# A hybrid decoder trunk on one core: other delays for the key and value compression, another share of filler products per head, and half of the small evictions on ScalarE

## The chip, the cores and the metric

The kernel runs on one core of one Trainium2 chip. The metric is the device time of one execution in microseconds (us). The kernel before takes 641.56 us, the median of three runs (640.89 to 641.58).

## The reference

Two layers over 256 tokens of width 1024, in float32. Layer 0 mixes a short convolution with latent attention, layer 1 is sparse attention with 16 heads in 4 groups; a squared-ReLU MLP follows each. The change touches the attention of layer 1, cut here to what matters:

```python
proj = xn @ w_in                       # q, and k/v of three branches, and gates
def compress(z, pe, w1, w2):           # blocks of 32 tokens, every 16
    blk = z[:, idx] + pe[:, None, :]
    hdn = jax.nn.gelu(jnp.einsum('bnlgd,lde->bnge', blk, w1))
    return hdn @ w2
kc, vc = compress(k_c, pe_k, w1_k, w2_k), compress(v_c, pe_v, w1_v, w2_v)
# each head: softmax over the 15 compressed blocks, over the selected blocks, over the window
out = g0 * softmax(q.kc - alibi) @ vc + g1 * softmax(q.ks - alibi) @ vs + g2 * softmax(q.kw - alibi) @ vw
return out @ w_out
```

With 256 tokens the 16 selected blocks are all four blocks there are, and the window covers everything, so those two branches are dense causal softmaxes.

## The kernel before

A dense product is three TensorE products: each operand is split into a high part (fp32r) and a low part, and high by high, high by low and low by high are summed in PSUM. A weight chunk (512 KB) is loaded by SP's queue into one of 4 `raw` buffers, its high part is copied by ScalarE (L170) and its low part subtracted by VectorE (L171), both into one of 5 `w` buffers.

TensorE's instructions run in the order in which the program issues them. That order is planned by hand with a clock (`tick`, L62): each product adds its planned duration (L91), 256 columns 109 ns. `defer(ns, fn)` (L75) puts a group of instructions off until the clock has moved on by that much; `need` (L83) forces what is still deferred when it is needed. The order on the other engines is chosen by the framework's scheduler; what stands in a `high_priority` block is preferred.

`mixer_c` (L671) is layer 1's attention. Four projections have their output turned (`turned_steps`, L349: a step is six products of 256 columns, 16 steps a projection, one epilogue two steps before the end, for the first half of the outputs, and one at the end): the keys (L821), the first query pair (L827), and then, as filler between the heads, "c" (the inputs of both compressions, L859) and "q" (the second query pair, groups 2 and 3, L860). After these the list of fillers holds the products of the output projection (`out_steps`), which wait for attention results.

- `epi_c(i)` (L774) scales the projection into `z[i]` (VectorE, L778), copies the lower half of the partitions to the upper half, one token on, by a DMA (L779), and defers `fold(i)`.
- `fold(i)` (L784) issues the compression's eight products (`compress`, L649, planned at 143 ns each), whose short chain on VectorE and ScalarE makes gelu's result (hk or hv), and defers `last_k` or `last_v`, the second product.
- `epi_q(1)` (L758) scales by VectorE (sp, L744) and writes the high and low parts of the queries qT (ScalarE L768, VectorE L769).

The head loop (L981) has 32 heads in slots 0 to 31, in units (gp, t) of eight heads: t is the half of the queries, t = 0 sees 128 keys, t = 1 sees 256. In a slot:

- `head_qk` (L895) makes the scores of both branches in one of two `sc` PSUM buffers; two fused passes on VectorE add the bias and take the maximum (L911), ScalarE exponentiates (L913), VectorE inverts the sum (L915), GpSimd scales (L918);
- what the table `at` holds for this slot: `scores_c` (L966, products with the compressed keys, then a chain of VectorE and ScalarE operations to the tile cpc, L1010 to L1027, and 6000 ns later by the clock the four transposes of cpc and ptc), `unit_pv` (L939, probabilities by values) and `unit_end` (L954, which forces the transposes of cpc of its unit and adds the compressed branch);
- `fill(FILL[i])` (L877): filler steps as long as the credit is positive; a debt is carried to the next slot, and credit that finds no filler ready is lost;
- `head_t` (L926): the transposes of the head four slots back, 2 blocks for t = 0 and 4 for t = 1, whose result is evicted from PSUM by VectorE for t = 0 (L935) and by ScalarE for t = 1 (L937).

The score chain of the first unit:

```python
s3 = ...                      # VectorE: reduce, add the bias, maximum, subtract
nc.scalar.activation(s3, s3, AF.Exp)
...                           # VectorE: sum, reciprocal, gate, scale
nc.scalar.activation(pc[:, :, 0:4:2, :], wide, AF.Copy)
nc.vector.tensor_tensor(pc[:, :, 1:4:2, :], wide, pc[:, :, 0:4:2, :].bitcast(F32), op=OP.subtract)
```

Of the kernel before, what the change touches and what calls it, by code (L numbers as in the profile page):

```python
# [39 lines left out]

LAG = 4
C_TILES = 2 * C_HEADS
FILL = (1900.0,) * 6 + (1200.0,) * 10 + (300.0,) * 5 + (700.0,) * 11 + (1200.0,) * 8


class Trunk:
# [624 lines left out]
    def mixer_c(self, x, rx, both, fin):  # L671
        nc, A = self.nc, self.A
        with ExitStack() as st:
# [16 lines left out]
            def wide(i):  # L690

                return rows[i].rearrange("p t n -> p (t n)")[:, None, :].to_broadcast([P, 2, 256])
# [81 lines left out]
            def epi_c(i, ps):  # L774
                with self.tc.high_priority():
                    for par in range(2):
                        rows_ = slice(64 * par, 64 * par + 64)
                        nc.vector.tensor_tensor(z[i][0:64, par:4:2, :], ps[rows_], wide(0)[rows_], op=OP.mult)  # L778
                    nc.sync.dma_start(z[i][64:128, 0:4, 0:S - 1], z[i][0:64, 0:4, 1:S])  # L779
                self.defer(5500.0 + 2500.0 * i, lambda: fold(i))  # L780

            cps = []

            def fold(i):  # L784
                if i == 0:
                    cps.append(self.acc(0))
                    self.compress(qp, cps[0][:, 0:80], z[0], w1[0], "ck", out_k)
                    self.defer(4500.0, last_k)
                else:
                    self.compress(qp, cps[0][:, 80:160], z[1], w1[1], "cv", out_v)  # L790
                    self.defer(4500.0, last_v)

            def out_k(xx, y):
                nc.vector.tensor_tensor(hk, xx, y, op=OP.mult)
# [62 lines left out]
            def always():  # L857
                return True
            fills = [("c", always, self.turned_steps(both, "c_in", 0, epi_c)),  # L859
                     ("q", always, self.turned_steps(both, "c_in", 3, epi_q(1))),  # L860
                     ("o", mixed(0, 0), out_steps(0, 0, (0, 1))),
# [15 lines left out]
            def fill(ns):  # L877
                credit[0] += ns
                while credit[0] > 0:
                    if not fills or not fills[0][1]():  # L880
                        credit[0] = 0.0
                        return
                    was = self.clk
                    step()
                    credit[0] -= self.clk - was
# [36 lines left out]
            def head_t(*a):  # L922
                with self.tc.high_priority():
                    head_t_(*a)

            def head_t_(gp, g, t, r, pb):  # L926
                n = 2 * (t + 1)
                if r == 0:
                    pts[g, t] = qp.tile([P, 4, 4, P], F32, name="pt", tag="pt", bufs=3)[:, 0:n]
                ph = pts[g, t]  # L930
                pt = self.trp()
                for b in range(n):
                    self.tr(pt[:, b, :], pb[:, b * P:(b + 1) * P])
                if t == 0:
                    nc.vector.tensor_copy(ph[:, :, r, :], pt[:, 0:n, :])  # L935
                else:
                    nc.scalar.activation(ph[:, :, r, :], pt[:, 0:n, :], AF.Copy)  # L937

            def unit_pv(gp, t):  # L939


                nb = t + 1
                y = yps[gp, t] = (self.acc(1) if (gp, t) != (1, 1) else
                                  pp.tile([P, 512], F32, name="sc", tag="sc", bufs=2))
                with self.tc.high_priority():
                    for b in range(2 * nb):
                        br, kb = b // nb, b % nb
                        for par in range(2):
                            self.mm(y[64 * par:64 * par + 64, :],
                                    vv[kb][:, br * 2 + gp, 64 * par:64 * par + 64],  # L950
                                    pts[2 * gp + par, t][:, b].rearrange("p a b -> p (a b)"), b == 0, False, 2,
                                    part=True)

            def unit_end(gp, t):  # L954

                with self.tc.high_priority():
                    self.need(lambda: (gp, t) in ptc)
                    self.mm(yps[gp, t], vcs[:, gp, :], ptc[gp, t], False, True, part=True)
                    mh, ml = self.xt_both(mixed_, gp, t)
                    y = yps[gp, t].rearrange("p (a b) -> p a b", a=4)  # L960
                    nc.scalar.activation(mh, y, AF.Copy)
                    nc.vector.tensor_tensor(ml, y, mh.bitcast(F32), op=OP.subtract)
                    mixT[t][gp] = (mh, ml)
                    ready[t, gp] = self.clk + 1500.0

            def scores_c(gp, t):  # L966
                self.need(lambda: left[0] == 2)
                fns = self.cmp_scores(qp, pp, [q and q[:, :, t] for q in qT], kc, cbias[:, t], gates[t], gp, t, ptc)
                self.defer(6000.0, fns[0])

            units = [(0, 0), (0, 1), (1, 0), (1, 1)]
            at = {}
            for u, i in enumerate((13, 16, 23, 29)):
                at.setdefault(i, []).append(lambda u=u: scores_c(*units[u]))
            for u in range(4):
                at.setdefault(8 * u + 8 + LAG, []).append(lambda u=u: unit_pv(*units[u]))
                at.setdefault(max(8 * u + 8 + LAG, 17), []).append(lambda u=u: unit_end(*units[u]))

            fill(2200.0)
            prob = {}  # L980
            for i in range(C_TILES + LAG + 4):  # L981
                now[0] = i
                if i < C_TILES:
                    gp, g, t, r = heads[i]
# [3 lines left out]
                for fn in at.get(i, []):  # L988
                    fn()
                fill(FILL[i])  # L990
                j = i - LAG
# [217 lines left out]
```

## Time and profile before

| | |
|---|---|
| median of three runs | 641.56 us |
| the profiled execution | 639.43 us, its span 637.6 us |
| TensorE busy | 617.9 us, 97% of the span |
| VectorE busy | 423.2 us, 66% |
| ScalarE busy | 375.0 us, 59% |
| GpSimd busy | 78.6 us, 12% |
| mean granted TensorE clock | 0.991 of full |

The profile names an engine (PE is TensorE, DVE VectorE, ACT ScalarE, POOL GpSimd, SPq SyncE's queue of DMA issues), the line of the kernel and the tiles that an instruction writes and reads (out<-in). Products that are issued by a helper all have its line (L92, L99, L104), so they are told apart by their tiles: acc<-z_k is the K compression, acc<-xth a filler product, sc<-qT a head's scores, sc<-kc the compressed scores, acc<-pt,vv the product of probabilities and values, tr<-cpc the transposes of the compressed probabilities. An instruction's duration on TensorE overlaps the next one's; the distance of two starts is what it costs. The attention of layer 1 begins near 320 us; its head loop runs from about 352 to 440.

### The profile page before, as it was taken

To read this page: it belongs to the slowest core of one execution; us is meant where nothing else is said; L and a number is where in the kernel's file an instruction comes from. 1 tells how busy PE (TensorE), PEld (TensorE's weight loads), DVE (VectorE), ACT (ScalarE), POOL (GpSimd) and SP (SyncE) were. 2 spreads that over 40 slices of the span, in tenths; PEclk is the share of its full clock that TensorE was granted. 3 is DMA by queue.
4 is the path that set the end of the run, shared out by engine and by line. 5 is a ranking of instruction groups with operands and counts; after the bars stand their busy time and mean duration, and the time that the engine had idled before them with its cause. 6 is when DMAs were issued, how large, how long until landed. Compare 5 with 4: busy or idle time off the path is not lost.

```text
span 637.6 us, 10525 instructions
## 1 busy us (share of the span) xinstructions
PE 617.9 (97%) x3712; PEld 536.6 (84%) x3712; DVE 423.2 (66%) x975; ACT 375.0 (59%) x860; POOL 78.6 (12%) x135
## 2 busy tenths in 40 slices
PE   7999999999999999999899897999999999999995
PEld 4889877889999988888899886776789999888884
DVE  6758797776676744445968789584966675644443
ACT  5786556756665644445857568596756565544431
POOL 1212330020000000000200535360300000000000
PEclk9999999999999999999999998999999999999998
DMA  8856336646556566566688814023636656556521
GB/s 279 292 180 218 129 101 197 219 146 199 185 178 197 168 208 192 194 198 211 198 271 262 219 47 133 1 68 106 222 105 206 190 174 203 188 193 198 197 69 66
DMA packets 33796, 111.67 MB, mean 175 GB/s; under 512 B 4240, under 2 KB 5328, under 8 KB 33744
## 3 DMA queue, kind: packets, MB, share of 16 engines
q1 hardware_dynamic: 33744, 111.01, 53.5%
q8 instruction: 29, 0.48, 0.3%
q14 instruction: 23, 0.19, 0.1%
HBM read 108.38 MB, written 1.05 MB: 172 GB/s over the span
## 4 chain that ended last, share of the span: by engine, by line
PE 60%; issue 28%; DVE 6%; ACT 2%; DMA 2%; POOL 1%; SPq 0%; DVEq 0%; POOLq 0%; ACTq 0%
PE acc L92 52%; PE sc L92 4%; PE tr L99 4%; DVE wlo L171 2%; ACT pbn L913 1%; DMA raw<-in_a_in 1%; DMA z_k<-z_k 1%; DVE xtl L254 1%; PE yp L92 1%; DVE X L292 1%; POOL rp L139 0%; DVE xlo L171 0%; DVE pst L282 0%; DVE pbn L911 0%; POOL rx L139 0%
## 5 line engine op out<-in xcount | busy, mean ns | idle before, releaser
L171 DVE TENSOR_TENSOR wlo<-raw,whi 128x512 fp32r<-128x512 f32 (+3 forms) x368 | 237.5, 683 | 127.1 <-ACT whi L170 125.0
L170 ACT ACTIVATE whi<-raw 128x512 fp32r<-128x512 f32 (+3 forms) x362 | 207.1, 617 | 139.8 <-PE acc L92 87.8
L92 PE MATMUL acc<-xtl,whi 128*128 128x256 f32 x512 | 143.8, 281 | 0.0
L92 PE MATMUL acc<-xth,whi 128*128 128x256 f32 x512 | 143.5, 280 | 0.0
L92 PE MATMUL acc<-xth,wlo 128*128 128x256 f32 x512 | 143.5, 280 | 0.0
L92 PE MATMUL acc<-whi,hl 128*128 128x512 f32 x256 | 99.8, 390 | 0.0
L92 PE MATMUL acc<-whi,hh 128*128 128x512 f32 x256 | 99.6, 389 | 0.0
L92 PE MATMUL acc<-wlo,hh 128*128 128x512 f32 x256 | 99.6, 389 | 0.0
L92 PEld LDWEIGHTS acc<-xth,whi 128*128 128x128 f32 x512 | 96.3, 188 | 1.0 <-issue 0.8
L92 PEld LDWEIGHTS acc<-xth,wlo 128*128 128x128 f32 x512 | 96.7, 189 | 0.1
L92 PEld LDWEIGHTS acc<-xtl,whi 128*128 128x128 f32 x512 | 96.2, 188 | 0.2
L92 PE MATMUL acc<-wlo,xth 128*128 128x512 f32 (+3 forms) x160 | 60.3, 379 | 1.3 <-DVE wlo L171 1.1
L92 PE MATMUL acc<-whi,xth 128*128 128x512 f32 (+3 forms) x160 | 60.3, 377 | 0.7 <-DVE whi L166 0.7
L92 PE MATMUL acc<-whi,xtl 128*128 128x512 f32 (+3 forms) x160 | 60.5, 378 | 0.0
L92 PEld LDWEIGHTS acc<-wlo,hh 128*128 128x128 f32 x256 | 48.1, 188 | 10.0
L92 PEld LDWEIGHTS acc<-whi,hl 128*128 128x128 f32 x256 | 48.1, 188 | 9.9
L92 PEld LDWEIGHTS acc<-whi,hh 128*128 128x128 f32 x256 | 48.1, 188 | 9.8
L139 POOL TENSOR_TENSOR rp<-mse,mhalf 128x1 f32<-128x1 f32 x8 | 5.1, 643 | 387.5 <-DVE mse L136 387.5
L918 POOL TENSOR_SCALAR pbn<-pbn,sm,gates 128x128 f32<-128x128 f32 (+1 forms) x64 | 39.6, 630 | 72.9 <-PE acc L92 39.8
L92 PEld LDWEIGHTS acc<-wlo,xth 128*128 128x128 f32 x160 | 30.0, 188 | 7.2 <-DVE wlo L171 2.7
L92 PEld LDWEIGHTS acc<-whi,xth 128*128 128x128 f32 x160 | 30.2, 189 | 5.6 <-ACT xth L252 1.1
L92 PEld LDWEIGHTS acc<-whi,xtl 128*128 128x128 f32 x160 | 30.1, 188 | 4.4
(237 smaller groups left out, 854.8 us busy)
## 6 DMA issues: line engine op xcount, KB each, us to landing
raw<-in_w SPq DMA_DIRECT2D x128, 512.0 KB, 4.3
raw<-in_c_in SPq DMA_DIRECT2D x16, 512.0 KB, 4.6
raw<-in_a_in SPq DMA_DIRECT2D x15, 512.0 KB, 4.5
raw<-in_a_out SPq DMA_DIRECT2D x8, 512.0 KB, 3.6
raw<-in_c_out SPq DMA_DIRECT2D x8, 512.0 KB, 3.9
raw<-in_a_qup SPq DMA_DIRECT2D x6, 384.0 KB, 3.5
gpost<-in_gpost SPq DMA_DIRECT2D x4, 512.0 KB, 3.8
bias<-in_bias SPq DMA_DIRECT2D x4, 512.0 KB, 4.1
```

Source lines behind the costliest of these rows:

```text
L92: self.nc.tensor.matmul(ps, a, b, start=start, stop=stop, **({"skip_group_check": True} if part else {}))
L99: self.nc.tensor.transpose(dst, src, self.ident)
L139: nc.gpsimd.tensor_tensor(r, e, self.mhalf, op=OP.pow)
L170: nc.scalar.activation(hi[:, sl], raw[:, sl], AF.Copy)
L171: nc.vector.tensor_tensor(lo[:, sl], raw[:, sl], hi[:, sl].bitcast(F32), op=OP.subtract)
L254: nc.vector.scalar_tensor_tensor(lo, src, gcol, hi.bitcast(F32), OP.mult, OP.subtract)
L292: nc.vector.scalar_tensor_tensor(self.X[t][:, sl], self.tmp.pop(0), r, self.X[t][:, sl], OP.mult, OP.add)
L913: nc.scalar.activation(pb[:, sl], pb[:, sl], AF.Exp, bias=nm[:, br:br + 1], scale=-1.0, accum_out=sm[:, br:br + 1])
L918: nc.gpsimd.tensor_scalar(pb[:, sl], pb[:, sl], sm[:, br:br + 1], gates[t][:, 1 + br, h:h + 1], OP.mult, OP.mult)
```

## The change

The planned delays from `epi_c` to the compressions grow from 5500 and 8000 ns to 8000 and 10300; those from a compression to its second product from 4500 to 5800 (K) and 5500 (V). The list of filler credits is 1500 for eight slots, 1250 for nine, 500 for four, and then as before, in place of 1900 for six, 1200 for ten and 300 for five. The first `scores_c` stands in slot 14 instead of 13, the first `unit_end` in slot 18 instead of 17. The evictions of t = 0 stay on VectorE for odd r and go to ScalarE for even r.

```diff
@@ -40,7 +40,7 @@
 
 LAG = 4
 C_TILES = 2 * C_HEADS
-FILL = (1900.0,) * 6 + (1200.0,) * 10 + (300.0,) * 5 + (700.0,) * 11 + (1200.0,) * 8
+FILL = (1500.0,) * 8 + (1250.0,) * 9 + (500.0,) * 4 + (700.0,) * 11 + (1200.0,) * 8
 
 
 class Trunk:
@@ -777,7 +777,7 @@
                         rows_ = slice(64 * par, 64 * par + 64)
                         nc.vector.tensor_tensor(z[i][0:64, par:4:2, :], ps[rows_], wide(0)[rows_], op=OP.mult)
                     nc.sync.dma_start(z[i][64:128, 0:4, 0:S - 1], z[i][0:64, 0:4, 1:S])
-                self.defer(5500.0 + 2500.0 * i, lambda: fold(i))
+                self.defer(8000.0 + 2300.0 * i, lambda: fold(i))
 
             cps = []
 
@@ -785,10 +785,10 @@
                 if i == 0:
                     cps.append(self.acc(0))
                     self.compress(qp, cps[0][:, 0:80], z[0], w1[0], "ck", out_k)
-                    self.defer(4500.0, last_k)
+                    self.defer(5800.0, last_k)
                 else:
                     self.compress(qp, cps[0][:, 80:160], z[1], w1[1], "cv", out_v)
-                    self.defer(4500.0, last_v)
+                    self.defer(5500.0, last_v)
 
             def out_k(xx, y):
                 nc.vector.tensor_tensor(hk, xx, y, op=OP.mult)
@@ -931,7 +931,7 @@
                 pt = self.trp()
                 for b in range(n):
                     self.tr(pt[:, b, :], pb[:, b * P:(b + 1) * P])
-                if t == 0:
+                if t == 0 and r % 2:
                     nc.vector.tensor_copy(ph[:, :, r, :], pt[:, 0:n, :])
                 else:
                     nc.scalar.activation(ph[:, :, r, :], pt[:, 0:n, :], AF.Copy)
@@ -970,11 +970,11 @@
 
             units = [(0, 0), (0, 1), (1, 0), (1, 1)]
             at = {}
-            for u, i in enumerate((13, 16, 23, 29)):
+            for u, i in enumerate((14, 16, 23, 29)):
                 at.setdefault(i, []).append(lambda u=u: scores_c(*units[u]))
             for u in range(4):
                 at.setdefault(8 * u + 8 + LAG, []).append(lambda u=u: unit_pv(*units[u]))
-                at.setdefault(max(8 * u + 8 + LAG, 17), []).append(lambda u=u: unit_end(*units[u]))
+                at.setdefault(max(8 * u + 8 + LAG, 18), []).append(lambda u=u: unit_end(*units[u]))
 
             fill(2200.0)
             prob = {}
```

## Rows read from the trace of the kernel before

**Rows 1.** waits of TensorE over the whole run: us in total, times, longest

```profile
PE tr L104 <- DVE cpc L1027: 2.4, 1, 2.4
PE acc L92 <- DMA z_k<-z_k: 2.0, 1, 2.0
...
PE sc L92 <- DVE nm L911: 0.9, 2, 0.6
PE acc L92 <- ACT ptc L1035: 0.7, 1, 0.7
...
PE acc L92 <- DVE cct L659: 0.7, 1, 0.7
```

**Rows 2.** busy us (x instructions) of each engine in five stretches, then PEclk, DMA share, GB/s

```profile
356.10:380.60 24.50, 21.79 (x167) 20.63 (x165) 19.48 (x80) 13.47 (x47) 9.11 (x15) 1.00 0.46 126
380.60:394.70 14.10, 10.73 (x71) 8.07 (x69) 13.53 (x51) 12.83 (x39) 7.48 (x11) 0.99 0.44 136
394.00:396.00 2.00, 0.75 (x4) 0.56 (x4) 1.77 (x10) 2.00 (x10) 1.71 (x3) 0.58 0.47 182
396.20:400.70 4.50, 4.50 (x20) 4.09 (x20) 2.77 (x15) 2.73 (x7) 1.19 (x3) 0.50 0.02 5
401.00:440.00 39.00, 39.00 (x200) 26.49 (x198) 24.65 (x100) 26.01 (x82) 16.02 (x28) 1.00 0.16 52
```

**Rows 3.** timeline of TensorE, 363 to 399 us: start us, us, instruction, [idle before it and its releaser]

```profile
363.99 2.46 PE L92 MATMUL acc<-z_k,cw 128*128 128x80 f32 x16 [1.99 <-DMA z_k<-z_k]
...
380.27 0.28 PE L92 MATMUL acc<-xth,wlo 128*128 128x256 f32 x1
...
381.17 2.05 PE L92 MATMUL acc<-pt,vv 128*64 128x512 f32 x8
...
384.67 0.60 PE L99 MATMUL tr<-ident,pbn 128*128 128x128 f32 x4
385.02 0.48 PE L92 MATMUL sc<-kTh,qT 128*128 128x512 f32 x1
...
385.57 0.96 PE L92 MATMUL sc<-kc,qT 128*128 128x32 f32 x8
386.38 0.66 PE L99 MATMUL tr<-ident,pbn 128*128 128x128 f32 x4
...
394.68 0.75 PE L104 MATMUL tr<-ident_r,cpc 128*128 128x128 f32 x4 [2.37 <-DVE cpc L1027]
...
396.71 1.05 PE L99 MATMUL tr<-ident,pbn 128*128 128x128 f32 x4
...
397.99 1.05 PE L99 MATMUL tr<-ident,pbn 128*128 128x128 f32 x4
```

**Rows 4.** timeline of VectorE, the query epilogue and the end of the score chain

```profile
382.04 0.69 DVE L744 TENSOR_TENSOR sp<-acc,row 128x512 f32<-128x512 f32 x1
...
383.50 1.60 DVE L769 TENSOR_TENSOR qT<-sp,qT 64x512 fp32r<-64x512 f32 x2
...
392.32 1.59 DVE L769 TENSOR_TENSOR qT<-sp,qT 64x512 fp32r<-64x512 f32 x2 [0.24 <-ACT qT L768]
...
394.21 0.42 DVE L1027 TENSOR_TENSOR cpc<-cs,cpc 128x256 fp32r<-128x256 f32 x1
```

**Rows 5.** timeline of the DMA queue (SyncE), the issue of the first z copy

```profile
358.11 0.65 SPq L779 DMA_DIRECT2D z_k<-z_k  x1
```

**Rows 6.** DMA issues by line, 320 to 420 us: times, KB each, median us to landing

```profile
z_k<-z_k SPq DMA_DIRECT2D x1, 255.0 KB, 5.8
```

**Rows 7.** groups of instructions by form, 356 to 396 us: busy us, mean ns | idle before

```profile
L913 ACT ACTIVATE pbn<-pbn,nm 128x256 f32<-128x256 f32 x16 | 8.0, 504 | 2.3 <-DVE nm L911 1.4 <-DVE sm L915 0.7
L171 DVE TENSOR_TENSOR wlo<-raw,whi 128x512 fp32r<-128x512 f32 x11 | 7.5, 690 | 0.3 <-ACT whi L170 0.3
...
L911 DVE CUSTOM_DVE_ANT_0 pbn<-sc,bias 128x256 f32<-128x256 f32 x16 | 6.3, 412 | 0.1
...
L935 DVE COPY pt<-tr 128x256 f32<-128x256 f32 x8 | 3.4, 419 | 1.1 <-PE tr L99 0.9
```

## The prediction

> **What bounds the kernel now.** I read the waits of TensorE first, since its order is written out by hand and it is the engine that is nearly always busy. Five of its waits lie close together, between 356 and 397 us, in the first half of layer 1's heads: 2.4 us for the last operation of the compressed-score chain (cpc), 2.0 for the copied z_k, 0.9 for a score buffer that VectorE still reads (twice), 0.7 for ptc, 0.7 for hk [rows 1]. The sum is 6.7 us. The windows then say which engine is short there [rows 2]: from 356.1 to 380.6 VectorE works 19.48 of 24.50 us, so it has 5.0 to spare; from 380.6 to 394.7 it works 13.53 of 14.10, ScalarE 12.83, and TensorE 10.73. The first waits are thus TensorE arriving too early with VectorE idle beside it; the last and longest is VectorE being late. There is a second cost: after the cpc wait the granted clock is 0.58 of full between 394 and 396 and 0.50 (1.2 GHz) until 400.7. From 401 to 440 TensorE is busy all 39.00 us [rows 2], so whatever is won before 401 is carried to the end.
>
> The timelines give the instants. The first z_k product waits 1.99 us until 363.99; the first half of the second query pair's products ends at 380.39; scores_c(0,0) runs from 385.57 to 386.38; the transposes of cpc begin at 394.68 after their 2.37 us of idleness [rows 3]. On VectorE the first query epilogue runs from 382.04 to 385.10, the second's last operation ends at 393.91, cpc at 394.63 [rows 4].
>
> **The order that the change makes.** A fill step is six 256-column products, planned at 109 ns each (256/2.4 + 2.5), 655 ns in all; a slot takes steps as long as its credit is positive and carries the debt on. After four steps ahead of the loop, slots 0 to 12 took 3,3,3,2,3,3,2,2,0,2,2,1,2 and slots 13 on nothing (28 steps; deferred groups charge their own time to the credit). With the new list slots 0 to 14 take 2,2,3,2,2,3,2,2,2,0,2,0,2,2,2. So head 4 is issued before the first compression epilogue instead of after, and heads 12 and 13, the first product of unit (0,0) and its four-transpose slot come before the first half of the second query pair ends. scores_c(0,0) goes from slot 13 to 14, the forced transposes of cpc from slot 17 to 18. By slot 15 the planned totals are equal again.
>
> **Cost, step by step**, against the profiled execution (639.43 us, span 637.6).
>
> *z_k.* TensorE stood before the compression at 362.0 (363.99 less 1.99 [rows 3]), which the plan puts 5.6 us after the epilogue's last product, so that product ended near 356.4; the copy was issued at 358.11 [rows 5] and took 5.8 us [rows 6], to 7.6 us after the product. Now 56 fill products, four heads and four pairs of transposes lie between, planned 8.1 us. The wait goes, with half a microsecond to spare: -2.0 there. Bounds: 0 (the copy is held on SP's in-order queue behind a c_out load that waits for a raw buffer) and -2.0; I take -2.0, since at 358.11 nothing held it.
>
> *hk.* Between the K compression and last_k the plan had 4.5 us and now has 5.9, against a wait of 0.7. It goes too: -0.7.
>
> *What these two are worth.* They are won at a place where VectorE is idle, and what ends last is VectorE at cpc. TensorE reached the end of the first query half at 380.4. It now has in front of that point the pv products of unit (0,0) (381.17 to 383.15, 2.0), two more four-block heads (385.02 to 385.57, 0.55 each) and one more slot of four transposes (384.67 to 385.02, 0.35) [rows 3], 3.45 us; head 4 falls out for a pair of transposes, 0.2 each way; the epilogue comes 0.2 later. 380.4 + 3.45 + 0.2 - 2.7 gives 381.4, hardly later than before. But more of VectorE's work is then behind it. Before, 13.5 us of work lay between there and cpc [rows 2]. Of that the second half of head 11's softmax, heads 12 and 13 (two passes of 0.41 each [rows 7], with a reciprocal some 0.9 a head) and one eviction of 0.42 are done by then: 2.3 us, using the 5.0 that were idle. 381.4 + 13.5 - 2.3 = 392.6 for cpc, against 394.63. A second way: the chain took from 386.38 to 394.63, 8.2 us, on a full VectorE; scores_c(0,0) now ends at 381.4 plus the rest of slot 13 and the head of 14 (eleven products 1.2, transposes 0.35, head 0.55, scores 0.81 [rows 3]), 384.3, and 384.3 + 8.2 = 392.5. Both say -2.1. TensorE without any wait would be there at about 389.1, so some 3.4 us of waiting stay.
>
> *One slot less behind the wait.* Head 13's transposes and head 18's scores, which ran from 396.71 to 397.99 at half clock [rows 3], now lie before it, in time that is idle anyway: -1.3.
>
> *Evictions.* Of the 16 copies of 0.42 us on VectorE [rows 7] eight go to ScalarE. There the nearest row is an exponential of 128x256, 504 ns [rows 7]; bounds 0.4 to 0.6 (the 128x512 eviction is under 0.6). Four of them fall in the stretch where ScalarE has 11 us free and VectorE 5, so they shorten nothing: 0. The other four fall after 401, where TensorE never waits: 0. If that cover failed, four late evictions would cost at most 2 us of pv(0,0)'s start. By the Trainium skill (TensorE: Matmul & The Clock Gate, section "Architectural detail") ScalarE works strictly first in, first out, so an eviction placed there stands behind exponentials that PE does not need yet; this speaks against the edit, and by it alone the sum would be up to 2 us worse. The stretch's free 11 us is why I keep 0.
>
> *New waits looked for.* Head 16 needs the first query epilogue: 4.7 us from its last product before, so 386.1 now, and TensorE gets to head 16 at about 386.9. Head 20 needs the second, 9.2 us before (384.7 to 393.91), so 394.6 now, and TensorE is at head 20 after 395. Both fit, the first barely. The SP queue gets no new transfer. The extra product steps in slots 23 and 28 come in a stretch without waits: 0.
>
> Sum: -2.1 - 1.3 = -3.4, of which the half-clock stretch stays. 639.43 becomes 636.0. The median of the runs, 641.56, stands 2.13 above the profiled execution, so I forecast 641.56 - 3.4, rounded: **638.2**. About 0.2%, or 1.3 us, is what a measurement of this kernel can tell from no change.
>
> **Rivals.** *All waits go.* If the chain is not held by VectorE's total but only by its place in the queue, cpc is ready at 389.1 and TensorE never stops: 5.6 us earlier, 0.7 from a slot that is gone at full clock, and the three slots to 400.7 at 2.4 instead of 1.2 GHz, some 2.7: -9.0, 632.6. For it: VectorE's 5.0 free us. Against it: even a VectorE without a gap from 381.4 on is not done before 392. The clock is what rows show: 1.00 through the 1.99 us wait, 0.50 after the cluster that ends in 2.37. The Trainium skill (same page, "What's actually happening") makes half speed the state of an idle array and full speed that of a busy one; the trace agrees.
>
> *The gain is eaten.* The c_out splits (0.69 each [rows 7]) are held back by weight buffers that the second query pair now keeps two slots longer. If four or five more halves than before come ahead of cpc, it ends 3 us later than I say, and what is left is under 1: 641.0.
>
> *Slower.* The score chain now starts with both query epilogues unfinished instead of one. Those epilogues themselves show what order alone costs: 4.7 us for the first, 9.2 for the second, 4.5 apart. If cpc is put behind such a pile and one c_out chunk more (1.4), it ends at 392.5 + 5.9 = 398.4, 3.8 later than before, less the 1.3: +2.5, 644.1. It decides from a cpc that ends after 397.2. For it: VectorE takes its work in order, and nothing in the chain is marked urgent. Against: it needs every pending operation ahead of the chain.
>
> **How the numbers follow.** My case 0.52, all waits gone 0.14, eaten 0.20, slower 0.14. My case with its bounds (z_k kept, or cpc 1.5 us sooner) runs from 636 to 640.3, so all of it is faster; with the second case that makes 0.66 faster, 0.20 same, 0.14 slower. The range takes in the case of no waits and the eaten one and leaves out most of the slower: 632.6 to 642.5.
>
> **What would show it.** Right: no wait for z_k and none for hk; cpc's wait between 2.5 and 4.5 us, ending near 392.5; granted clock at a half behind it; VectorE over 20 us busy between 356 and 381. Wrong: a wait for qT before head 16, z_k still waited for, cpc later than 395, or no dip of the clock at all.

## The result and the profile after

The changed kernel takes 637.43 us (median of 4 runs, 637.01 to 638.28) beside 641.57 for the kernel before in the same runs: a ratio of 0.9938, 95% interval 0.992 to 0.9955, 4.1 us by the medians. The forecast was 638.2. The profiled execution is 637.01 us, its span 635.0.

The profiles of this study differ by up to 2.7 us in when layer 1 is reached, which the change doesn't touch, so I read a **stage time** that leaves that out: from the GpSimd power in layer 1's pre-norm to the first power in its post-norm. From there to the last such power it is 186.9 us in every profile, so what a change in the heads does is in this time. GpSimd's timeline of the kernel before, and of the changed one:

```profile
309.28 1.52 POOL L139 TENSOR_TENSOR rx<-mse,mhalf 128x1 f32<-128x1 f32 x1 [5.78 <-DVE mse L136]
...
445.67 0.93 POOL L139 TENSOR_TENSOR rp<-mse,mhalf 128x1 f32<-128x1 f32 x1 [14.79 <-DVE mse L136]
```

```profile
310.00 1.53 POOL L139 TENSOR_TENSOR rx<-mse,mhalf 128x1 f32<-128x1 f32 x1 [5.78 <-DVE mse L136]
...
443.06 0.93 POOL L139 TENSOR_TENSOR rp<-mse,mhalf 128x1 f32<-128x1 f32 x1 [13.30 <-DVE mse L136]
```

136.39 us before and 133.06 after: the stage won 3.33 us, where the prediction had 3.4. A stage time comes from one profiled execution; the two kernels that were profiled twice repeat within 0.2 and 0.4 us (E9, E10). The waits of TensorE after, the rows that answer to [rows 1]:

```profile
PE sc L92 <- DVE nm L911: 2.9, 2, 1.9
...
PE tr L104 <- DVE cpc L1027: 0.9, 1, 0.9
PE acc L92 <- ACT ptc L1035: 0.7, 1, 0.7
```

The waits for z_k and ahead of the products that read hk are gone from the list. cpc fell from 2.4 to 0.9, but the waits for a score buffer grew from 0.9 to 2.9. The sum of these five went from 6.7 to 4.5 us. The windows, columns as in [rows 2] (busy us and instructions of PE, PEld, DVE, ACT, POOL, then the clock):

```profile
356.10:380.60 24.50, 24.50 (x174) 21.06 (x173) 20.63 (x85) 17.37 (x60) 13.02 (x21) 1.00 0.50 156
380.60:394.70 14.10, 10.29 (x78) 9.33 (x77) 13.26 (x51) 13.06 (x39) 5.40 (x9) 0.89 0.26 81
392.00:396.00 4.00, 1.90 (x7) 1.45 (x8) 3.46 (x19) 3.49 (x15) 2.59 (x6) 0.50 0.38 132
396.20:400.70 4.50, 4.50 (x22) 3.30 (x22) 2.83 (x15) 3.70 (x12) 0.95 (x3) 0.74 0.02 4
401.00:440.00 39.00, 39.00 (x204) 27.35 (x201) 23.78 (x91) 27.24 (x80) 14.16 (x25) 1.00 0.17 55
```

TensorE is now busy without a gap from 356 to 380.6, and VectorE does 20.63 us there instead of 19.48. From 380.6 to 394.7 VectorE and ScalarE are as full as before (13.26 and 13.06 of 14.10) and TensorE does less (10.29). The granted clock still falls to half, once, but earlier against the work. TensorE's timeline in the full stretch, and VectorE's:

```profile
383.35 0.96 PE L92 MATMUL sc<-kc,qT 128*128 128x32 f32 x8
...
388.37 1.03 PE L92 MATMUL sc<-kc,qT 128*128 128x32 f32 x8 [0.98 <-DVE nm L911]
...
392.50 0.55 PE L92 MATMUL sc<-kTh,qT 128*128 128x256 f32 x1 [1.91 <-DVE nm L911]
...
394.18 0.75 PE L104 MATMUL tr<-ident_r,cpc 128*128 128x128 f32 x4 [0.92 <-DVE cpc L1027]
...
398.77 3.65 PE L92 MATMUL acc<-pt,vv 128*64 128x512 f32 x14
```

```profile
384.50 1.41 DVE L769 TENSOR_TENSOR qT<-sp,qT 64x512 fp32r<-64x512 f32 x2
...
386.15 0.41 DVE L1011 TENSOR_REDUCE cs<-sc 128x128 f32<-128x256 f32 x1
...
390.00 1.67 DVE L769 TENSOR_TENSOR qT<-sp,qT 64x512 fp32r<-64x512 f32 x2
...
391.98 0.16 DVE L1022 TENSOR_TENSOR csm<-csm,gates 128x8 f32<-128x8 f32 x1
...
392.27 0.29 DVE L1023 TENSOR_TENSOR cs<-cs,csm 128x128 f32<-128x128 f32 x1
...
393.63 0.50 DVE L1027 TENSOR_TENSOR cpc<-cs,cpc 128x256 fp32r<-128x256 f32 x1
```

cpc ends at 394.13, 84.13 us into the stage; before it was 85.35 into it [rows 3, 4]. So cpc came 1.2 us sooner, not 2.1. The first product of unit (0,1) starts at 398.77, 88.77 into the stage; before it started at 400.68, which is 91.40: 2.6 sooner. The last 0.7 came later still, and the experiments say from where.

In the table, each ratio is to runs of the kernel before on the same chip, whose medians were 641.49 us for E1 to E4, 640.99 for E5 to E8 and 640.13 for E9 to E12.

| kernel | stage, us | median, us | ratio to before, 95% |
|---|---|---|---|
| before | 136.39 | 641.57 | 1 |
| changed | 133.06 | 637.43 | 0.9938 (0.992 to 0.9955) |
| E1 delays alone | 134.70 | 638.67 | 0.9967 (0.9953 to 0.998) |
| E2 fillers alone | 134.02 | 638.37 | 0.9949 (0.9928 to 0.997) |
| E3 evictions alone | 138.32 | 639.66 | 0.9983 (0.9958 to 1.0008) |
| E4 changed, no evictions | 133.77 | 638.23 | 0.9954 (0.9936 to 0.9972) |
| E5 changed, slots of before | 132.24 | 635.25 | 0.9911 (0.988 to 0.9941) |
| E6 changed, unit_end in 19 | 135.09 | 638.49 | 0.9971 (0.995 to 0.9993) |
| E7 changed, query part on GpSimd | 135.29 | 638.6 | 0.996 (0.994 to 0.998) |
| E8 changed, c_out copies on GpSimd | 133.80 | 637.75 | 0.9953 (0.9932 to 0.9974) |
| E9 changed, again | 133.24 | 637.54 | 0.9949 (0.9927 to 0.997) |
| E10 = E5, again | 131.85 | 635.35 | 0.9916 (0.989 to 0.9942) |
| E11 = E5, second scores in 17 | 131.26 | 634.81 | 0.9906 (0.988 to 0.9932) |
| E12 = E5, no evictions | 132.65 | 636.23 | 0.9947 (0.9922 to 0.9972) |

### The profile page after: what moved, and what is told of

It reads as the page before. It is cut to its first block, busy times and chain, and to the rows that moved or that the text cites. A ratio compares the mean times of both kernels' runs of the same rounds, so it can differ in the third digit from the quotient of the medians.

```text
span 635.0 us, 10535 instructions
## 1 busy us (share of the span) xinstructions
PE 617.4 (97%) x3712; PEld 535.0 (84%) x3712; DVE 420.8 (66%) x967; ACT 377.2 (59%) x868; POOL 78.1 (12%) x135
## 4 chain that ended last, share of the span: by engine, by line
PE 63%; issue 28%; DVE 5%; DMA 1%; ACT 1%; POOL 1%; SPq 0%; DVEq 0%; POOLq 0%; ACTq 0%
PE acc L92 54%; PE sc L92 5%; PE tr L99 4%; DVE wlo L171 1%; DMA raw<-in_a_in 1%; DVE xtl L254 1%; PE yp L92 1%; DVE X L292 0%; DVE xlo L171 0%; POOL rp L139 0%; POOL rx L139 0%; PE tr L104 0%; DVE pst L282 0%; DVE qT L769 0%; ACT qT L768 0%
```

## The experiments

**E1, the delays alone.**

```diff
-                self.defer(5500.0 + 2500.0 * i, lambda: fold(i))
+                self.defer(8000.0 + 2300.0 * i, lambda: fold(i))
...
-                    self.defer(4500.0, last_k)
+                    self.defer(5800.0, last_k)
...
-                    self.defer(4500.0, last_v)
+                    self.defer(5500.0, last_v)
```

> Only the four longer delays, fillers, slots and evictions as before. The stage time is read from the GpSimd power of layer 1's pre-norm (309.28 before, 310.00 after) to the first power of its post-norm (445.67 before, 443.06 after): 136.39 us before, 133.06 after, a gain of 3.33. Theory A (VectorE sets the end of the score chain; a removed TensorE wait counts only as far as VectorE is fed earlier): z_k and hk are no longer waited for, but cpc ends less than 1.5 us sooner and its wait grows, stage 135.0 to 136.5. Rival B (the delays are the change: each removed wait counts in full): stage 133.7, 2.7 us shorter.

Measured: stage 134.70, 1.7 us won. The waits for z_k and ahead of the products that read hk are gone as both theories had it, a new wait of 1.0 us for hv takes part of it back, and the wait for cpc grew from 2.4 to 3.5.

```profile
PE tr L104 <- DVE cpc L1027: 3.5, 1, 3.5
PE acc L92 <- DVE hv L798: 1.0, 1, 1.0
```

cpc ended 83.8 into the stage, 1.6 sooner. That is between A (under 1.5, stage 135.0 or more) and B (133.7): removing the early waits counts for more than A allowed and for less than their sum.

**E2, the fillers alone.**

```diff
-FILL = (1900.0,) * 6 + (1200.0,) * 10 + (300.0,) * 5 + (700.0,) * 11 + (1200.0,) * 8
+FILL = (1500.0,) * 8 + (1250.0,) * 9 + (500.0,) * 4 + (700.0,) * 11 + (1200.0,) * 8
```

> Only the new list of filler credits. Theory A: the heads reach VectorE earlier and fillers last to slot 14, so the stage is 1 to 2.5 us shorter even though z_k is still waited for by 1.5 to 2.5 us: 134 to 135.4. Rival B: the waits for z_k and hk stay, so nothing is won: 136.4.

Measured: 134.02, 2.4 us won, in A's range, though this profile has the clock at half twice between the heads (374.0 to 377.4 and 394.5 to 397.9). cpc ended 82.5 into the stage, 2.8 sooner than before, and is not waited for. But A's condition is wrong: z_k is not waited for either. TensorE's timeline and the DMA issue of z_k in this kernel:

```profile
364.62 2.38 PE L92 MATMUL acc<-z_k,cw 128*128 128x80 f32 x16
...
373.97 0.65 PE L92 MATMUL acc<-hk,w2k 64*128 64x60 f32 x2 [1.15 <-issue]
```

```profile
z_k<-z_k SPq DMA_DIRECT2D x1, 255.0 KB, 3.0
```

With the old delay the compression starts at 364.62 without a wait, since the copy took 3.0 us instead of 5.8 [rows 6]. The changed kernel's copy took 3.0 too. SP's queue, of the kernel before and of the changed one, shows what differs. The last load ahead of the copy follows for each, with its size and its time from issue to landing.

```profile
350.63 6.49 SPq L159 DMA_DIRECT2D raw<-in_c_out  x4
```

```profile
351.53 4.67 SPq L159 DMA_DIRECT2D raw<-in_c_out  x3
359.66 0.65 SPq L779 DMA_DIRECT2D z_k<-z_k  x1
...
362.78 10.62 SPq L159 DMA_DIRECT2D raw<-in_c_out  x4
```

```profile
raw<-in_c_out SPq DMA_DIRECT2D x1, 512.0 KB, 6.3
```

```profile
raw<-in_c_out SPq DMA_DIRECT2D x1, 512.0 KB, 4.3
```

Before, four c_out loads of 512 KB were issued ahead of z_k. The last of them, issued at 356.80, landed at 363.08, so it was under way for 5.0 of the copy's 5.8 us [rows 5, 6]. Now three are, and the last, issued at 355.87, landed at 360.15, 0.5 us after the copy's issue. In E1 and E3, with four loads ahead, the copy took 4.9 and 6.0 us and landed 0.9 and 1.6 us after the fourth load; in every other profile three stand ahead and it took 3.0. The fourth load has fallen behind the copies: it is issued at 362.78, as a weight split on VectorE ends (362.72), where before it was issued at 356.80, as one ended (356.77). That the split comes later because "c" advances more slowly and its weight buffers come free later is only argued. So there were two ways to end this wait, and the change takes both. The 2.4 us of this run thus hold the end of the z_k wait as well as the heads that come earlier, and no run separates the two.

The wait ahead of the products that read hk, 1.15 us, stays in E2 and is gone in E1: that one is the delay's. In E2 it is a wait for hk, which ends at 373.87. In the kernel before it was not:

```profile
372.94 0.43 PE L92 MATMUL acc<-hk,w2k 64*128 64x60 f32 x2 [0.65 <-DVE cct L659]
```

```profile
369.55 0.23 DVE L794 TENSOR_TENSOR hk<-ccx,ccy 64x60 f32<-64x60 f32 x1
...
372.67 0.22 DVE L659 TENSOR_TENSOR cct<-acc,ccs 64x75 f32<-64x75 f32 x1
```

hk was done 3.2 us ahead. The products write into the accumulator of the V compression, and they waited until VectorE had read that compression's result out of it (cct).

**E3, the evictions alone.**

```diff
-                if t == 0:
+                if t == 0 and r % 2:
```

> Only the eight evictions on ScalarE. My step put this at 0: stage 136.1 to 136.7. Rival C (VectorE is short everywhere, so 1.7 us less of its work before cpc shortens the stage): 135.0 or less. By the rule of strict order on ScalarE it could be longer, up to 138.

Measured: stage 138.32, 1.9 us longer, while the medians say 0.9983 with 1 in the interval. The profiled execution, 643.47 us, lies 3.8 above the median of its kernel. TensorE's row for z_k in this run, and the window behind it:

```profile
366.56 3.06 PE L92 MATMUL acc<-z_k,cw 128*128 128x80 f32 x16 [2.63 <-DMA z_k<-z_k]
```

```profile
367.60:371.00 3.40, 3.40 (x19) 3.40 (x18) 1.01 (x7) 0.89 (x4) 0.00 (x0) 0.50 0.38 148
```

z_k was waited for by 2.63 us instead of 1.99, and directly behind that the granted clock was 0.50 from 367.6 to 371.0 (1.2 GHz), with TensorE busy all along. In the profiled execution of the kernel before the clock held at 1.00 behind its wait of 1.99 us at this place [rows 2]. By an estimate from these rows the 3.4 us at half clock cost up to 1.7 and the longer wait 0.6, and scores_c ended 79.3 into the stage, already 2.1 later than before. This stage time is therefore no measure of the evictions, and the run leaves them open; E4 and E12 settle them.

**E4 and E12, the change without the evictions, and E5 without them.**

```diff
-                if t == 0 and r % 2:
+                if t == 0:
```

> The changed kernel with all evictions of t = 0 back on VectorE. Theory A: these fall where VectorE has time, stage 132.9 to 133.5 as with them on ScalarE (133.06). Rival C: VectorE has 1.7 us more before cpc, stage 134 to 135.

> The same with all evictions of t = 0 on VectorE (so: delays and fillers alone, on the slots of before). The evictions were worth 0.7 us in the changed kernel (133.77 without them). If that holds on any order: stage 132.8 to 133.2, median about 636. If they count only where VectorE runs the score chain last: 132.1 to 132.4.

Measured: 133.77 against 133.06, and 132.65 against 132.24 and 131.85. The evictions are worth 0.7 in one order and 0.4 to 0.8 in the other (0.8 against E10, whose clock was at half for as long as E12's, 3.4 us): more than my 0, less than C's 1 to 2; both runs fall between the ranges expected. Of this, 0.3 to 0.4 has come about by the first product of unit (0,1). Some 0.4 more is seen in one place, behind 401, where I had said that TensorE never waits. The product of unit (1,0) before, VectorE's rows around it, the same product after with VectorE's last copy, and the product in E4:

```profile
418.62 2.45 PE L92 MATMUL acc<-pt,vv 128*64 128x512 f32 x8
```

```profile
417.90 0.86 DVE L171 TENSOR_TENSOR wlo<-raw,whi 128x512 fp32r<-128x512 f32 x1
418.68 0.41 DVE L935 COPY pt<-tr 128x256 f32<-128x256 f32 x1
```

```profile
416.59 2.05 PE L92 MATMUL acc<-pt,vv 128*64 128x512 f32 x8
```

```profile
416.23 0.42 DVE L935 COPY pt<-tr 128x256 f32<-128x256 f32 x1
```

```profile
415.93 2.53 PE L92 MATMUL acc<-pt,vv 128*64 128x512 f32 x8
```

Eight products take 2.05 us in all nine profiles with the change's evictions and 2.44 to 2.53 in the five with every eviction of t = 0 on VectorE. The last head's copy (odd r) is on VectorE in all of them; what differs is what stands ahead of it there. With all evictions on VectorE it stands behind a weight split (417.90) and starts 0.4 to 0.5 us after the transposes that it copies have ended, and the second product starts only as the copy ends (419.10 and 419.09). With the neighbour's copy on ScalarE no split stands there, and it starts within 0.05 us of the transposes. Why the scheduler puts no split there then is not shown. The list of waits and the 39.00 of 39.00 us of [rows 2] don't show this: the products' ends are modelled, so a group that waits in its middle counts as busy.

**E5 and E10, the slots of before.** Only the two slots of the change are taken back.

```diff
-            for u, i in enumerate((14, 16, 23, 29)):
+            for u, i in enumerate((13, 16, 23, 29)):
...
-                at.setdefault(max(8 * u + 8 + LAG, 18), []).append(lambda u=u: unit_end(*units[u]))
+                at.setdefault(max(8 * u + 8 + LAG, 17), []).append(lambda u=u: unit_end(*units[u]))
```

> The changed kernel with the first compressed scores in slot 13 and the first unit_end in slot 17 again. My step: one slot of transposes and scores (1.3 us at half clock) goes behind the wait again, and the score chain starts 2 us earlier by the plan. If VectorE's total sets the chain's end, the chain gains less than the slot costs: stage 133.5 to 135 against 133.06. If the chain's end is set by when it starts, it is shorter: 132 to 133.

> The changed kernel with the slots of before (scores in 13, unit_end in 17), again, in more rounds, beside the changed kernel on one chip. If the slots cost what the first run showed (stage 132.24 against 133.06, median 635.25 against 637.43), it is 1 to 2.5 us faster than the changed kernel; if that was chance, within 0.6 us of it.

Measured: 132.24 and 131.85; the medians 635.25 and 635.35, the second beside 637.54 for the changed kernel on the same chip (E9). This part of the change, both slots together, costs about 2 us of the median; no run moves only one of them. VectorE's timeline and TensorE's waits in E5:

```profile
381.85 0.42 DVE L1011 TENSOR_REDUCE cs<-sc 128x128 f32<-128x256 f32 x1 [0.25 <-PE sc L92]
...
385.20 1.40 DVE L769 TENSOR_TENSOR qT<-sp,qT 64x512 fp32r<-64x512 f32 x2
...
389.43 0.42 DVE L1027 TENSOR_TENSOR cpc<-cs,cpc 128x256 fp32r<-128x256 f32 x1
...
391.07 1.40 DVE L769 TENSOR_TENSOR qT<-sp,qT 64x512 fp32r<-64x512 f32 x2 [0.62 <-ACT qT L768]
```

```profile
PE sc L92 <- DVE nm L911: 1.2, 1, 1.2
...
PE sc L92 <- DVE csm L1019: 0.5, 1, 0.5
```

The chain now begins at 381.85, before either query epilogue, and cpc ends at 389.85: 80.45 into the stage, 3.7 us sooner than in the changed kernel, and TensorE no longer waits for it. Two things make up the 3.7. On TensorE scores_c, a slot earlier, ends 72.4 into the stage instead of 74.3. And on VectorE the first reduction follows at once, where in the changed kernel it starts 1.8 us after the end of scores_c (384.31), behind the first query epilogue. The low parts of the second query epilogue, in the changed kernel inside the chain (390.00), now follow cpc (391.07).

The chain's length varies less than its start: from its first reduction to the end of cpc it takes 7.5 us before (387.09 to 394.63), 8.0 in the changed kernel (386.15 to 394.13), 8.0 here, and from 7.5 to 8.7 over all fourteen profiles. During the 8.0 us VectorE is busy 7.74 here and 7.54 in the changed kernel, ScalarE 6.49 and 7.62; so a ScalarE with more idle time did not make it shorter. What sets its end is mainly when it starts. The stage kept only 0.8 of the 3.7 us: TensorE still waits for a score buffer, and the clock falls here too. The two profiles of this kernel differ by 0.4 us, with the clock at half for 6.8 us in one (389.8 to 396.6) and 3.4 in the other (392.0 to 395.4).

**E6, unit_end in slot 19.**

```diff
-                at.setdefault(max(8 * u + 8 + LAG, 18), []).append(lambda u=u: unit_end(*units[u]))
+                at.setdefault(max(8 * u + 8 + LAG, 19), []).append(lambda u=u: unit_end(*units[u]))
```

> The changed kernel with the first unit_end one slot later still (19). The 0.9 us wait for cpc goes behind one more slot and vanishes. If the waits for score buffers are the same shortage of VectorE under another name, they grow and little is won: stage 132.2 to 133.1. If cpc was a wait of its own, 0.9 and the slot's share at half clock count: 131.5 or less.

Measured: 135.09, 2.0 us longer than the changed kernel, outside both.

```profile
PE sc L92 <- DVE nm L911: 3.3, 3, 1.9
...
PE acc L92 <- ACT ptc L1035: 1.0, 1, 1.0
```

```profile
400.06 5.75 PE L92 MATMUL acc<-pt,vv 128*64 128x512 f32 x14
```

The wait for cpc is gone and came back as 0.4 more for score buffers and 0.3 more for ptc; and the clock stayed at half from 394.1 to 404.3, where the changed kernel had it from 391.7 to 398.6. The first product of unit (0,1) starts 88.7 into the stage, as in the changed kernel (88.8); the 2.0 us are lost behind it, where fourteen products take 5.75 us instead of 3.65 with the clock still at half. The profiled execution, 640.38 us, lies 1.9 above the median; the medians differ by 0.9 to 1.1 us (638.49 against 637.54 and 637.43). So nothing is won by waiting elsewhere; why the clock stayed low for longer isn't settled.

**E7, the low part of group 3's queries on GpSimd.**

```diff
-                            nc.vector.tensor_tensor(l, s_, h.bitcast(F32), op=OP.subtract)
+                            (nc.gpsimd if (j, b) == (1, 1) else nc.vector).tensor_tensor(
+                                l, s_, h.bitcast(F32), op=OP.subtract)
```

> The changed kernel with the low part of group 3's queries (two operations on VectorE, 1.67 us, between 390.0 and 391.7) made on GpSimd. Theory A (VectorE's total ahead of cpc sets the end): the wait for a score buffer before head 18 shrinks from 1.9 to under 0.8 and cpc ends over 1 us sooner, stage 131 to 132.2. Rival D (ScalarE, 13.06 of 14.10 us busy, or the order sets it): 132.8 to 133.3. If GpSimd's own scaling of the heads is held up: over 133.3.

Measured: 135.29, over every theory but the last, and not for its reason: no wait of TensorE is put down to GpSimd's scaling. The wait for the buffer shrank to 0.43, as A had it, and cpc came later, 85.1 into the stage. Two operations of the chain on VectorE, and GpSimd's rows:

```profile
390.39 1.28 DVE L1023 TENSOR_TENSOR csm<-csm,gates 128x8 f32<-128x8 f32 x1
...
392.19 1.35 DVE L1024 TENSOR_TENSOR cs<-cs,csm 128x128 f32<-128x128 f32 x1
```

```profile
390.37 3.02 POOL L769 TENSOR_TENSOR qT<-sp,qT 64x512 fp32r<-64x512 f32 x2
```

(The lines have moved by one.) In the changed kernel the same two take 0.16 and 0.29 us; here 1.28 and 1.35, during GpSimd's 3.02 us. Taking 1.67 us of work off VectorE put 2.2 us onto it, and cpc came 1.0 later. Of the 2.2 us that the stage lost, 0.9 had come about by the first product of unit (0,1); the rest is the clock, at half until 401.8, so that its fourteen products took 5.01 us instead of 3.65. The run therefore tells nothing about VectorE's total; it shows the price of using both engines at once.

**E8, the high parts of c_out chunks 1 and 2 on GpSimd.**

```diff
-                    out_cs[cg, c] = self.chunk(A["c_out"][cg, c], 2, 512)
+                    out_cs[cg, c] = self.chunk(A["c_out"][cg, c], 2, 512, pool_hi=(cg, c) in ((0, 1), (0, 2)))
```

> The changed kernel with the high parts of c_out chunks 1 and 2 (four copies of 0.6 us) made on GpSimd in place of ScalarE. Theory A: ScalarE is not what is short, stage 132.8 to 133.3. Rival D (ScalarE sets the end as much as VectorE): 2.4 us less of ScalarE's work in the full stretch, stage under 132.3.

Measured: 133.80, outside both ranges and 0.7 over the changed kernel, the median nearly the same (637.75). The waits keep their sizes (score buffers 3.2, cpc 0.8). Of the 0.7, 0.45 is the clock, at half 1.0 us into unit (0,1)'s products. The edit did not do what its expectation says: of the four copies two ran on GpSimd early (366.60 to 368.23) and only two in the full stretch (388.05 to 389.25), and ScalarE is busy 12.56 of the 14.10 us that answer to 380.6 to 394.7, instead of 13.06. So the run speaks against rival D but doesn't decide it; E5's chain, as long with a less busy ScalarE, is the better evidence.

**E9, the changed kernel again.**

> The changed kernel again, beside the next on one chip. Its stage was 133.06 us. If stage times repeat but for the stretches of half clock, this profile gives 133.06 within 0.2 when its clock falls once between the heads, as before, and 1 to 2 us more when it falls twice. Median 637 to 638.

Measured: 133.24, median 637.54. The stage repeats within 0.2 where the clock falls in the same way.

**E11, the second unit's scores one slot later as well.**

```diff
-            for u, i in enumerate((13, 16, 23, 29)):
+            for u, i in enumerate((13, 17, 23, 29)):
```

> The same with the second unit's compressed scores one slot later (17 instead of 16), so that head 16's scores do not share the two score buffers with them. If place in the queue decides, the 1.24 us wait in slot 16 shrinks and the stage is 131.2 to 132.0. If the wait is VectorE's shortage, it moves to the next head: 132.0 to 132.5. If the second chain is now late for its own transposes in slot 20: over 132.5.

Measured: 131.26, median 634.81, the fastest kernel of the study, 0.5 under E10 beside it; the runs of the two overlap (633.99 to 634.96, and 634.43 to 635.64).

```profile
PE sc L92 <- DVE nm L911: 1.6, 3, 0.8
```

The wait of 1.24 us became 0.80 and 0.48: it is split between the heads more than it is removed, and TensorE does not wait for the second chain's cpc.

## Why the prediction was right, and where it was not

The size was right, 3.4 forecast and 3.33 in the stage, and so were the direction and the place. Both sources of the gain that it had in mind are there: the early waits end (E1: 1.7 us), and heads move ahead of fillers while VectorE has time (E2: 2.4 us, the end of the z_k wait included). But that the size is right to 0.1 is luck. Of the two terms of the sum, cpc gave 0.9 us less than forecast and the slot what was forecast, and 0.7 came after the first product of unit (0,1), where the sum had nothing.

**z_k** (-2.0 there): the wait went, as forecast, but not by the delay alone. I held the copy's 5.8 us fixed, and with one load less ahead of it it took 3.0.

**hk** (-0.7): the wait went, as forecast, but I had read it wrongly. It was a wait for the V compression's accumulator to be read (372.89); hk itself had ended at 369.78.

**cpc** (-2.1): 1.2 measured. The work of the first way, 13.5 - 2.3 = 11.2 us, was about right for the changed kernel. From the end of the first query half (382.44) to the end of cpc VectorE is busy 10.91 us (columns as in [rows 2]); but it is idle for 0.8 of that time, and the half ended 0.3 later than forecast. The same stretch of E5, from its 383.16 on, follows:

```profile
382.44:394.13 11.69, 7.93 (x60) 7.04 (x58) 10.91 (x43) 10.80 (x32) 4.83 (x8) 0.90 0.28 90
```

```profile
383.16:389.85 6.69, 4.91 (x38) 4.31 (x36) 6.50 (x28) 5.93 (x15) 2.02 (x4) 0.99 0.21 78
```

What failed is the reading that all of this work must lie ahead of cpc: in E5 only 6.50 us of it do. The second way, the chain from the end of scores_c, missed as well. scores_c ended 74.3 into the stage, 0.7 sooner than the forecast 384.3 (75.0), but cpc came 9.8 us after that instead of 8.2: the first reduction starts 1.8 us after scores_c, behind the first query epilogue, where before it was 0.6 (386.53 to 387.09), and the chain took 8.0 instead of 7.5. So the wait for cpc, forecast at 2.5 to 4.5, was 0.9; the waiting came earlier, at the score buffers, and the three waits between scores_c and cpc (0.98, 1.91 and 0.92) make 3.8, near the 3.4 that the prediction had left.

**One slot less behind the wait** (-1.3): measured against the changed kernel's own cpc it is there, 2.6 less 1.2. But the sum had no term for what the other half of that edit does: scores_c in slot 14 starts behind a query epilogue. E5, without both halves, is 0.8 to 1.4 us of stage and 2 us of median better. The two slots together, which I counted as a gain, were a loss.

**Evictions** (0): worth 0.4 to 0.8 (E4, E12). The cover that I named for those after 401, "TensorE never waits", was a modelled busy time. Some 0.4 of the 0.7 us that the stage won after the first product of unit (0,1) is this; another 0.2 is the clock, which was back at full when that product began (398.77), and before at half until 401.1, 0.4 us after its start (400.68).

**The rivals.** "All waits go" was rejected because a full VectorE can't be done before 392. E5 has cpc at 389.85: so the place in the queue does move it that far, about half by an earlier scores_c and half by VectorE's order. But the waits don't all go there: three stay that sum to about 2 us, the clock still falls, and the median is 635.3, not 632.6. "The gain is eaten" and "slower" did not come. ScalarE in strict order did not show a price: E4 and E12 give the evictions a gain, and E3's loss is the clock's and the longer wait's. As forecast, head 16 did not wait for qT, and the dip of the clock stayed.

**The median against the profile.** The medians differ by 4.1 us, the stages by 3.3. Of the 66 runs of the kernel before beside the experiments, 20 had a mean clock of 0.991 or more and lie from 637.0 to 640.3 us, as its profiled execution does (639.43), and 46 had less and lie from 639.8 to 644.0; the changed kernel's 16 runs have 0.989 to 0.992 and lie from 636.7 to 638.6. E3's profile shows one way to lose clock that the change removes, the stretch behind the wait for z_k; that it is the way in each of those 46 isn't shown.

## What to carry to other kernels

A wait at one place can be the shortage of an engine at another; read which engine is idle before the wait and which is full behind it, and then ask for the order in the full engine's queue, not only its total. Here a chain through VectorE and ScalarE took 7.5 to 8.7 us wherever it stood, so its start was worth more than work taken off an engine: issue such a chain ahead of bulk work that isn't needed yet (E10 and E11 beat the change, E9, by 2.2 and 2.7 us of the median on one chip). When fillers are respread, look at which transfers then stand ahead of others in the DMA queue: here a copy that nobody had touched took half the time with one load less ahead of it. And when an operation moves to another engine, look at what is then ahead of those that stay: that was the gain of the evictions behind 401.

## What was not expected of the hardware

VectorE's operations on two tiles in SBUF took 1.28 and 1.35 us instead of 0.16 and 0.29 while GpSimd read SBUF (E7). The Trainium skill (SBUF — State Buffer, section "Who interferes with whom") says that a VectorE instruction with two SBUF inputs contends with a GpSimd instruction that reads SBUF, for a pair of ports that is an exclusive lock; the trace agrees: the two operations end at 391.67 and 393.54, within 0.15 us of the GpSimd operations beside them (391.64 and 393.39).

The clock fell to half with small waits: in E5 the two before the fall were 0.54 and 1.24 us. In the kernel before it held through a single 1.99 us. In E3 it fell after 2.63, and stayed at half for 3.4 us in which TensorE was busy throughout.

A SBUF to SBUF copy of 255 KB took 3.0, 4.9, 5.8 or 6.0 us, with no change in itself: 3.0 with three loads issued ahead of it, the rest with four, of which the last was still under way for most of the copy's time and landed 0.9 to 1.6 us before it.
